# State-space columns from the scaled input while the shift vector loads, and B matrices loaded by group

## The chip, the core and the metric

The kernel runs on one core of a Trainium2 chip as one launch. The metric is the device time of one execution, in microseconds (us); less is better. The engines go by their short names: PE is TensorE (matmuls and transposes; PEld its weight loads), DVE is VectorE, ACT is ScalarE, POOL is GpSimd, and SP is SyncE, which issues most of the DMAs. Weights lie in HBM in f32 and are read through SBUF; matmuls write to PSUM.

## The reference

Two transformer blocks for 256 tokens of width 2048. The change touches the first. Its input is normalised, scaled by `1 + sc1` and shifted by `sh1`; both vectors are a product of the condition vector with 2048 columns of `w_ada`. The projection `w_in` gives u (1024 columns, for the state-space branch), then q, k, v and two gates. Cut to that:

```python
mod = c_act @ w_ada[l] + b_ada[l]
sh1, sc1, g1, sh2, sc2, g2 = [m[:, None, :] for m in jnp.split(mod, N_MOD, axis=-1)]
h = rms_norm(x, norm_mix_g[l]) * (1.0 + sc1) + sh1
proj = h @ w_in[l]
u, q, k, v, ga, gb = jnp.split(proj, split_at, axis=-1)
y_ssm = s5_branch(u, ...)       # per group of 16 columns: B u, a diagonal recurrence over 256 tokens, C s, GLU
y_att = moba_attention(q, k, v, rel_bias)
merged = sigmoid(ga) * (y_ssm @ w_proj_ssm[l]) + sigmoid(gb) * (y_att @ w_proj_attn[l])
x = x + g1 * (merged @ w_out[l])
h2 = rms_norm(x, norm_mlp_g[l]) * (1.0 + sc2) + sh2
x = x + g2 * (jnp.square(jax.nn.relu(h2 @ w_ff1[l])) @ w_ff2[l])
```

The state-space branch has 64 groups with 64 states and 16 columns each; its B matrices `ssm_b_re` and `ssm_b_im` are 64 x 64 x 16.

## The kernel before

**Layout.** Activations stand transposed, features on the 128 partitions and the 256 tokens along a row, in 16 chunks of 128 features. `xT` (two tiles of 8 chunks, in pairs `xp`) is the input so.

**GEMMs.** `gemm` walks the 2048 rows of a weight in steps of 4 chunks by 512 columns: one 1 MB tile `w` per step. `piece` loads it and splits it in two f32r parts, `wh` by ACT (a rounding copy) and `wl` by DVE (the rest). The activations are split in the same way (`h1h`, `h1l`; for the GLU `zhh`, `zhl`). Each product is three matmuls (high by high, high by low, low by high) into PSUM tiles `ga` or `gb`, which ACT evicts (`store_pairs`).

**Conditioning vectors.** `ada_pe` computes one on PE: 16 chunks of 1 MB (`aw`), each times the condition vector repeated over 32 columns (`crep`), four matmuls of 512 columns a chunk, which the hardware runs as eight, into `adap`. `ada` does the same on DVE, in an accumulator `acc`. `ada_fin` copies the sum (`adae`), transposes it (`adat`) and adds bias and gain into `mod`.

**Order.** Up to `pinned[0] = False` (L921) each engine keeps the program's order. From there the tile scheduler orders by its own simulation of the engines. Work beside the GEMMs stands in two lists of generators: `work` (state space, attention) and `stream` (later conditioning vectors). After each part of a GEMM step `bg(dve, ada)` gives credits, 3.6 us of DVE work and 0.65 of a chunk per step of 4 chunks (`TUNE` d1 and r1), and takes the next pieces of the two lists.

**The prologue.** SP issues the chunks of sc1 (`g_sc1`). After the tenth chunk's place in the queue stand the two B loads (L317) and two C loads (L320) into `ssrc`, with runs of 16 f32 for B. `x_in` transposes x on PE (`xt`), DVE copies it to `xT`; the sum of squares gives `rstd`. `ssm_prep` computes the state-space coefficients (`ws`, transposed in `ptp` to `prm`), then rotation tables 0, 1 and 2 (`ssm_table`, doubling steps ln = 1 to 64 into `tab`) with `ssm_blocks` for the four column pairs (`bd`, `cd`, transposed in `pb` and `pc` to `bct`) behind table 0. `columns` brings gains and biases into `colT`. `rr` is the relative-position bias, `bf` its reversed form. After sc1 come the 16 chunks of sh1, during which `mod_scale` writes `xT` times sc1 and rstd; then `mod_shift` makes `h1`.

**The main phase.** The GEMMs follow: u in two halves of 512 columns (L946), q, k, v, a gate, the attention projection, the other gate, and the GLU of the state-space output. `ssm()` starts behind u (L949): for each of 16 pairs of tiles PE makes `bu` from `uT` and `bct`, DVE rotates it with the table, scans along the tokens and rotates back (`wr`, `wi`, `p`), PE sums over the states into `yp`, DVE adds to `uT`, and ACT applies gelu and splits it to `zhh`.

Of the kernel before, what the change touches and what calls it, by code (L numbers as in the profile page):

```python
# [79 lines left out]
def tile_kernel(ctx: ExitStack, tc: tile.TileContext, I, out):  # L80
# [40 lines left out]
    def unit(shape, name="u", dt=F32):  # L121
        return up.tile(shape, dt, name=nm(name), tag="U")

    def scr(shape, name="s", dt=F32):
        return sp.tile(shape, dt, name=nm(name), tag="S")

    def tiny(shape, name="t", dt=F32):
        return tp.tile(shape, dt, name=nm(name), tag="T")
# [6 lines left out]
    def pmisc(shape, name="m"):  # L135
        return psb.tile(shape, F32, name=nm(name), tag="B")
# [175 lines left out]
    g_sc1 = ada_pe(1, 1, "norm_mix_g", crep, pacc_, True)  # L312
    src = unit([P, 4, 512], "ssrc")

    def load_src():
        for k, n in enumerate(("ssm_b_re", "ssm_b_im")):
            SY.dma_start(src[:, k, :].rearrange("p (t q) -> p t q", t=32),  # L317
                        I[n][0].rearrange("(t g) n q -> (g n) t q", g=2))
        for k, n in enumerate(("ssm_c_re", "ssm_c_im")):
            SY.dma_start(src[:, 2 + k, :].rearrange("p (c n) -> p c n", c=8),  # L320
                        I[n][0].rearrange("(c g) q n -> (g q) c n", c=8))
# [105 lines left out]

    def mod_scale(xp, rstd, a, c, dst):
        V.scalar_tensor_tensor(dst, xp[c // 2][:, c % 2, :], a[:, c:c + 1], rstd, op0=OP.mult, op1=OP.mult)

    def mod_shift(t, sh, c, hl):
        S.activation(hl.hi(c), t, AF.Identity, bias=sh[:, c:c + 1])
        V.scalar_tensor_tensor(hl.lo(c), t, sh[:, c:c + 1], hl.hi(c).bitcast(F32),
                               op0=OP.add, op1=OP.subtract)

    def modulate(xp, rstd, a, sh, hl, keep=None, then=None):
        n, ts, lag = 2 * len(xp), {}, 3
        for i in range(n + lag):
            if i < n:
                ts[i] = scr([P, L], "mt") if keep is None else keep[i // 8][:, i % 8, :]  # L440
                mod_scale(xp, rstd, a, i, ts[i])
            c = i - lag
            if c >= 0:
                mod_shift(ts[c], sh, c, hl)
                if c in (3, 7) and then is not None:
                    then()

# [166 lines left out]
    def ssm_prep():  # L614
# [64 lines left out]
        V.tensor_copy(prm, pt)  # L679
        yield 0.2  # L680
        yield from ssm_table(0)
        for pp in range(2):
            bc = unit([P, 2, 2, 512], "bct")
            for k in range(2):
                cp2 = 2 * pp + k
                bct[cp2] = [bc[:, k, i, :].rearrange("p (r c m) -> p r c m", r=2, c=2) for i in range(2)]
                yield from ssm_blocks(cp2, src)
        for cp2 in range(1, 3):
            yield from ssm_table(cp2)

# [182 lines left out]
    xp = pairs_of(xT)  # L873
    r0 = []

    def x_in():
        st = tiny([P, 2], "xst")
        junk = unit([P, D], "xsq")
        for t in range(2):
            S.activation(junk, xtok[t], AF.Square, accum_out=st[:, t:t + 1])  # L880
        for c2 in range(8):
            pt = pmisc([P, 2, L], "xt")
            for k in range(2):
                for t in range(2):
                    T.transpose(pt[:, k, t * P:(t + 1) * P],
                                xtok[t][:, (2 * c2 + k) * P:(2 * c2 + k + 1) * P], ident)
            V.tensor_copy(xp[c2], pt)
            yield 0.6
        r = rsqrt_of(st, 1.0 / D, 2)
        yield 1.0  # L890
        rs = scr([P, L], "rstd")
        S.copy(rs, spread([r[:, t:t + 1] for t in range(2)], pmisc([P, L], "rows")))
        r0.append(rs)
        yield 0.1

    g_x = start(x_in())
    g_ssm = start(ssm_prep())
    g_col = None
    for i, _ in enumerate(g_sc1):
# [8 lines left out]
        bg(2.5, 0)  # L908
    rstd = r0[0]
    start(moba_flip())  # L910
    h = HL(16, "h1")
    for i, _ in enumerate(ada_pe(1, 0, None, crep, pacc_, True)):
        if i < NC:
            mod_scale(xp, rstd, mods[(1, 1)], i, xp[i // 2][:, i % 2, :])
        bg(2.3, 0)
    pre = []
    for c in range(NC):
        mod_shift(xp[c // 2][:, c % 2, :], mods[(1, 0)], c, h)
        if c in (3, 7):
            pre.append(piece(I["w_in"][0], c - 3, 4, 0, 512))  # L920
    pinned[0] = False  # L921

    def queue_ada(*specs, pe=False):
# [9 lines left out]

    w_in = I["w_in"][0]
    for j, g_ in ((2, None), (4, "norm_mlp_g"), (3, None), (5, None)):
        queue_ada((1, j, g_), pe=str(j) in TUNE["pe"])

    def store_pairs(dst, base, func=AF.Copy, scale=1.0):
# [3 lines left out]
        return ev  # L942

    uT = unit([P, 8, L], "uT")
    for nb in range(2):
        gemm(w_in, NC, nb * 512, [("A", 512, store_pairs([uT], 4 * nb))], h, rate=TUNE["r1"], dve=TUNE["d1"], pre=pre if nb == 0 else ())  # L946

    drain(g_ssm)
    g_ssm = start(ssm())  # L949

# [59 lines left out]
    for nb in range(2):  # L1010
        gemm(w_in, NC, 1024 + nb * 512, [("A", 512, store_pairs([qT], 4 * nb, scale=SCALE))], h, rate=TUNE["r1"], dve=TUNE["d1"])
    for nb in range(2):
# [66 lines left out]
    def then(w, n0=0, nn=512):  # L1079
        return lambda: pre.append(piece(w, 4 * len(pre), 4, n0, nn)) if len(pre) < 2 else None  # L1080
# [742 lines left out]
```

## Time and profile before

| | |
|---|---|
| time, median of 3 runs | 3319.54 us (3318.26 to 3321.86) |
| the profiled execution | 3320.44 us |
| its span in the trace | 3318.7 us |
| mean granted PE clock | 0.975 |
| busy: PE, DVE, ACT, POOL | 89%, 68%, 29%, 25% of the span |
| read from HBM | 1064 MB, 321 GB/s over the span |

The first block takes about the first third of the span. [...] A stage is read by what has no idle time in it; an engine's idle time elsewhere costs nothing. Durations of neighbours on one engine overlap by a little, so that from start to start they are shorter than the duration shown.

### The profile page before, as it was taken

The numbers are of one execution on the slowest core, as the hardware profiler recorded it, in microseconds if no ns is written. First come the engines' busy times: TensorE is split into PE (matmuls) and PEld (weight loads), VectorE is DVE, ScalarE is ACT, GpSimd is POOL, SyncE is SP. The second block draws the span as 40 slices with busy tenths as digits, with TensorE's granted clock in tenths as the row PEclk, the third lists the DMA queues.
The fourth block names the chain that finished last, engine by engine and source line by source line (L and its number), as shares of the span: only waits on it lengthen the run. The fifth ranks groups of instructions, "written<-read, shape, count | busy, mean of one in ns | idle before, by whom it ended". The sixth has DMA issues, their size and how long they took to land.

```text
span 3318.7 us, 39085 instructions
## 1 busy us (share of the span) xinstructions
PE 2966.0 (89%) x15580; PEld 2151.7 (65%) x15580; DVE 2268.4 (68%) x3360; ACT 951.7 (29%) x1271; POOL 817.5 (25%) x540
## 2 busy tenths in 40 slices
PE   6899999999999999999999998988877768777777
PEld 2687889998998889997999886444322223222222
DVE  7687689877788888877766647545655565555642
ACT  1323433444443343345336731111111101111000
POOL 1000000000000000000000005556666666666663
PEclk8899999999999999999999998999999989999999
DMA  9866667877899999984883448999999999999998
GB/s 367 303 224 212 208 228 239 300 273 241 285 328 336 328 335 328 328 288 155 280 273 115 153 165 358 419 418 420 421 422 421 422 422 421 422 421 421 422 421 340
DMA packets 280459, 1068.90 MB, mean 322 GB/s; under 512 B 27380, under 2 KB 35991, under 8 KB 189525
## 3 DMA queue, kind: packets, MB, share of 16 engines
q1 hardware_dynamic: 202306, 524.35, 45.8%
q0 software_dynamic: 74752, 538.26, 39.1%
q10 hardware_dynamic: 3220, 3.81, 0.4%
q8 instruction: 122, 2.00, 0.2%
q14 instruction: 59, 0.48, 0.0%
HBM read 1064.24 MB, written 2.11 MB: 321 GB/s over the span
## 4 chain that ended last, share of the span: by engine, by line
PE 61%; DMA 29%; DVE 5%; issue 2%; POOL 1%; ACT 1%; SPq 0%; POOLq 0%; ACTq 0%; DVEq 0%
PE ga L94 31%; DMA dn<-in_peer_down_dram,eid 24%; PE gb L94 18%; PE pe L94 4%; DMA up<-in_peer_up_dram,eid 3%; DVE dn L94 2%; PE adap L94 2%; DMA aw<-in_w_ada_dram 2%; PE xt L94 1%; PE bu L94 1%; PE yp L94 1%; PE wqp L94 1%; PE o L94 1%; DMA up<-in_peer_up_dram,er 1%; POOL dn L1689 1%
## 5 line engine op out<-in xcount | busy, mean ns | idle before, releaser
L94 PE MATMUL pe<-up,cdg 128*128 128x512 f32 x1792 | 831.7, 613 | 258.9 <-DMA up<-in_peer_up_dram,eid 189.4
L1689 POOL DMA_INDIRECT dn<-in_peer_down_dram,eid x256 | 499.4, 1951 | 2256.4 <-DVE g L94 1969.3
L94 DVE SCALAR_TENSOR_TENSOR dn<-dn,htok 128x2048 f32<-128x2048 f32 x256 | 586.0, 2291 | 482.5 <-DMA dn<-in_peer_down_dram,eid 482.4
L94 PEld LDWEIGHTS pe<-up,cdg 128*128 128x128 f32 x1792 | 336.5, 195 | 744.0 <-issue 510.7
L94 ACT ACTIVATE wh<-w 128x2048 fp32r<-128x2048 f32 (+1 forms) x284 | 538.9, 1897 | 876.3 <-PE ga L94 488.5
L94 DVE TENSOR_TENSOR wl<-w,wh 128x2048 fp32r<-128x2048 f32 (+1 forms) x284 | 643.1, 2265 | 193.0 <-ACT wh L94 144.2
L1689 POOL DMA_INDIRECT up<-in_peer_up_dram,eid x224 | 266.5, 1190 | 155.6 <-issue 51.5
L94 DVE SCALAR_TENSOR_TENSOR acc<-aw,cT,acc 128x2048 f32<-128x2048 f32 x105 | 246.6, 2348 | 48.1 <-DMA aw<-in_ada_w_dram 29.9
L94 PE MATMUL ga<-h2h,wh 128*128 128x256 f32 x1024 | 249.1, 283 | 0.0
L94 PE MATMUL ga<-h2l,wh 128*128 128x256 f32 x1024 | 248.6, 283 | 0.0
L94 PE MATMUL ga<-h1h,wh 128*128 128x256 f32 x896 | 224.1, 289 | 0.0
L94 PE MATMUL ga<-h1l,wh 128*128 128x256 f32 x896 | 220.4, 284 | 0.0
L94 PE MATMUL gb<-wh,ah 128*128 128x512 f32 x512 | 199.6, 390 | 0.0
L94 PE MATMUL gb<-wh,al 128*128 128x512 f32 x512 | 199.4, 390 | 0.0
L94 PEld LDWEIGHTS ga<-h2h,wh 128*128 128x128 f32 x1024 | 196.5, 192 | 1.9 <-issue 1.7
L94 PEld LDWEIGHTS ga<-h2l,wh 128*128 128x128 f32 x1024 | 196.5, 192 | 0.2
L94 PEld LDWEIGHTS ga<-h1h,wh 128*128 128x128 f32 x896 | 172.7, 193 | 19.5 <-issue 15.3
L94 ACT ACTIVATE cdg<-ca,cf 128x128 f32<-128x128 f32 x224 | 77.0, 393 | 356.4 <-PE pe L94 345.9
L94 PEld LDWEIGHTS ga<-h1l,wh 128*128 128x128 f32 x896 | 172.9, 193 | 0.9 <-issue 0.8
L94 PE MATMUL ga<-h2h,wl 128*128 128x256 f32 x1024 | 134.1, 283 | 0.0
L94 PE MATMUL ga<-h3l,wh 128*128 128x256 f32 x528 | 132.1, 288 | 0.0
L94 PE MATMUL ga<-h3h,wh 128*128 128x256 f32 x528 | 132.0, 288 | 0.0
(444 smaller groups left out, 4327.4 us busy)
## 6 DMA issues: line engine op xcount, KB each, us to landing
w<-in_w_ff_dram SPq DMA_DIRECT2D x128, 1024.0 KB, 6.6
w<-in_w_in_dram SPq DMA_DIRECT2D x100, 1024.0 KB, 5.6
aw<-in_w_ada_dram SPq DMA_DIRECT2D x96, 1024.0 KB, 7.2
aw<-in_ada_w_dram SPq DMA_DIRECT2D x96, 1024.0 KB, 6.3
w<-in_w_out_dram SPq DMA_DIRECT2D x32, 1024.0 KB, 5.1
wq<-in_peer_wq_dram SPq DMA_DIRECT2D x16, 1024.0 KB, 10.2
w<-in_w_proj_attn_dram SPq DMA_DIRECT2D x8, 1024.0 KB, 5.0
w<-in_w_proj_ssm_dram SPq DMA_DIRECT2D x8, 1024.0 KB, 5.7
```

The costliest lines, as they stand in the source:

```text
L94: r = f(*a, **k)
L1689: r = G.indirect_dma_start(out=rows_, out_offset=None, in_=table, in_offset=bass.IndirectOffsetOnAxis(ap=idx, axis=0))
```

## The change

1. **B matrices.** Both are loaded by group into `raw` (64 partitions, 4 KB contiguous in each). 32 f32 matmuls for each, against a permuted identity, move it to the layout of `ssrc` in PSUM (`sb`), and an ACT copy brings it there.
2. **Input.** `rstd` is computed first and multiplied in when `xt` is taken from PSUM. `mod_scale` is gone.
3. **sh1** (`ada_both`): even chunks are accumulated by DVE (`acc`), odd ones on PE; a product of `acc` with ones adds the two.
4. **u** is taken while sh1 loads: eight 1 MB tiles `wu` of `w_in`'s first 1024 columns, in f32, times `xT` scaled by sc1 and not yet shifted. The f32r GEMM of u is gone.
5. **`u_shift`**, at the head of `stream`: the same columns are loaded again in eight tiles and multiplied by the shift vector `shrep`; the 1024 sums are added to `uT` by ACT.
6. `ssm_prep` makes tables 0 and 1 only; `ssm()`, which makes the others, starts behind q. During q the stream's rate is 1.0.

```diff
+    raw = unit([64, 2, 1024], "raw")
 
     def load_src():
         for k, n in enumerate(("ssm_b_re", "ssm_b_im")):
-            SY.dma_start(src[:, k, :].rearrange("p (t q) -> p t q", t=32),
-                        I[n][0].rearrange("(t g) n q -> (g n) t q", g=2))
+            SY.dma_start(raw[:, k, :], I[n][0].rearrange("g n q -> g (n q)"))
...
-    def mod_scale(xp, rstd, a, c, dst):
-        V.scalar_tensor_tensor(dst, xp[c // 2][:, c % 2, :], a[:, c:c + 1], rstd, op0=OP.mult, op1=OP.mult)
...
+        par = ident[0:64, 0:64].rearrange("p (t g) -> p g t", g=2)
+        for k in range(2):
+            ps = pmisc([P, 32, 16], "sb")
+            rv = raw[:, k, :].rearrange("g (n q) -> g n q", q=16)
+            for q in range(16):
+                for g in range(2):
+                    T.matmul(ps[64 * g:64 * g + 64, :, q], rv[:, :, q], par[:, g, :], start=True, stop=True,
+                             skip_group_check=True)
+            S.copy(src[:, k, :], ps.rearrange("p t q -> p (t q)"))
+            yield 0.1
         yield from ssm_table(0)
...
-        for cp2 in range(1, 3):
-            yield from ssm_table(cp2)
+        yield from ssm_table(1)
...
+        r = rsqrt_of(st, 1.0 / D, 2)
+        rs = scr([P, L], "rstd")
+        S.copy(rs, spread([r[:, t:t + 1] for t in range(2)], pmisc([P, L], "rows")))
+        yield 1.0
...
-            V.tensor_copy(xp[c2], pt)
+            V.tensor_mul(xp[c2], pt, rs.unsqueeze(1).to_broadcast([P, 2, L]))
...
+    uT = unit([P, 8, L], "uT")
+    def ada_both(blk, j, g):
+        dest = const([P, 16], "mod")
+        ps = pacc_([P, 512], "adap")
+        acc = unit([P, D], "acc")
+        for kc in range(NC):
+            wt = rot_tile("aw")
+            SY.dma_start(wt, adaw[blk][kc * P:(kc + 1) * P, j * D:(j + 1) * D])
+            if kc == 0:
+                V.tensor_scalar(acc, wt, ccol[blk][:, 0:1], None, op0=OP.mult)
+            elif kc % 2 == 0:
+                V.scalar_tensor_tensor(acc, wt, ccol[blk][:, kc:kc + 1], acc, op0=OP.mult, op1=OP.add)
+            for l, r in [(crep[:, kc, :], wt)] * (kc % 2) + [(ones[:, 0:32], acc)] * (kc == NC - 1):
+                for q in range(4):
+                    T.matmul(ps[32 * q:32 * q + 32, :], l, r[:, 512 * q:512 * q + 512], start=(kc == 1),
+                             stop=(r is acc), skip_group_check=True)
+            yield 0.0
+        ada_fin(blk, j, ps, dest, g)
+        yield 0.2
+    g_sh1 = ada_both(1, 0, None)
+    def u_load(nb, k):
+        wt = rot_tile("wu").rearrange("p (c n) -> p c n", c=4)
+        SY.dma_start(wt, w_in[4 * k * P:(4 * k + 4) * P, nb * 512:nb * 512 + 512]
+                     .rearrange("(c p) n -> p c n", p=P))
+        return wt
+    for i in range(8):
+        nb, k = divmod(i, 4)
+        wt = u_load(nb, k)
+        if k == 0:
+            ups = [pmisc([P, 2, L], "up") for _ in range(2)]
+        for d in (0.3, 2.3):
+            next(g_sh1)
+            bg(d, 0)
+        if i == 7:
+            for _ in g_sh1:
+                pass
+        for kk in range(4):
+            c = 4 * k + kk
+            if nb == 0:
+                xx, a_ = xp[c // 2][:, c % 2, :], mods[(1, 1)][:, c:c + 1]
+                if kk % 2:
+                    S.activation(xx, xx, AF.Copy, scale=a_)
+                else:
+                    V.tensor_scalar(xx, xx, a_, None, op0=OP.mult)
+            for j in range(4):
+                T.matmul(ups[j // 2][:, j % 2, :], wt[:, kk, j * P:(j + 1) * P], xp[c // 2][:, c % 2, :],
+                         start=(c == 0 and j % 2 == 0), stop=(c == NC - 1), skip_group_check=True)
+        if nb == 0 and k == 3:
+            for j in range(2):
+                S.copy(uT[:, 2 * j:2 * j + 2, :], ups[j])
     h = HL(16, "h1")
-    for i, _ in enumerate(ada_pe(1, 0, None, crep, pacc_, True)):
-        if i < NC:
-            mod_scale(xp, rstd, mods[(1, 1)], i, xp[i // 2][:, i % 2, :])
-        bg(2.3, 0)
     pre = []
     for c in range(NC):
         mod_shift(xp[c // 2][:, c % 2, :], mods[(1, 0)], c, h)
         if c in (3, 7):
-            pre.append(piece(I["w_in"][0], c - 3, 4, 0, 512))
+            pre.append(piece(w_in, c - 3, 4, 1024, 512))
...
+    def u_shift():
+        rep = scr([P, NC, 32], "shrep")
+        V.tensor_copy(rep, mods[(1, 0)].unsqueeze(2).to_broadcast([P, NC, 32]))
+        ps = pmisc([P, 512], "adap")
+        for k in range(8):
+            wt = wp.tile([P, 2, 1024], F32, name=nm("wu"), tag="W")
+            SY.dma_start(wt, w_in[2 * k * P:(2 * k + 2) * P, 0:1024].rearrange("(c p) n -> p c n", p=P))
+            for c in range(2):
+                for q in range(2):
+                    T.matmul(ps[32 * (2 * c + q):32 * (2 * c + q) + 32, :], rep[:, 2 * k + c, :],
+                             wt[:, c, 512 * q:512 * q + 512], start=(k == 0), stop=(k == 7),
+                             skip_group_check=True)
+            yield 0.0
+        ev = scr([P, 512], "adae")
+        S.copy(ev, ps)
+        pt = pmisc([P, 4, P], "adat")
+        for b in range(4):
+            T.transpose(pt[:, b, :], ev[:, 128 * b:128 * b + 128], ident)
+        two = tiny([P, 2, 2, 4], "us")
+        V.tensor_copy(two, pt.rearrange("p b (c q r) -> p c q b r", c=2, q=2)[:, :, :, :, 0])
+        b8 = tiny([P, 8], "ub")
+        V.tensor_add(b8.rearrange("p (q b) -> p q b", q=2), two[:, 0], two[:, 1])
+        for c in range(8):
+            S.activation(uT[:, c, :], uT[:, c, :], AF.Identity, bias=b8[:, c:c + 1])
...
+    g_us = u_shift()
+    stream.append(g_us)
...
-    uT = unit([P, 8, L], "uT")
-    for nb in range(2):
-        gemm(w_in, NC, nb * 512, [("A", 512, store_pairs([uT], 4 * nb))], h, rate=TUNE["r1"], dve=TUNE["d1"], pre=pre if nb == 0 else ())
-
-    drain(g_ssm)
-    g_ssm = start(ssm())
...
-        gemm(w_in, NC, 1024 + nb * 512, [("A", 512, store_pairs([qT], 4 * nb, scale=SCALE))], h, rate=TUNE["r1"], dve=TUNE["d1"])
+        gemm(w_in, NC, 1024 + nb * 512, [("A", 512, store_pairs([qT], 4 * nb, scale=SCALE))], h, rate=1.0,
+             dve=TUNE["d1"], pre=pre if nb == 0 else ())
+    drain(g_us, g_ssm)
+    g_ssm = start(ssm())
```

On PE in the prologue, before (`xt` are the transposes of x, `adap` a chunk of sc1, `rr` the position bias):

```order
L94 MATMUL ptp_283<-ca_81,ws_130 128x32 x5
L94 MATMUL xt_290<-ca_81,xtok_85 128x128
...
L94 MATMUL adap_142<-aw_315,crep_96 32x512 x4
L94 MATMUL xt_321<-ca_81,xtok_85 128x128
...
L94 MATMUL rr_341<-hot_98,rb_100 8x512
L94 MATMUL xt_348<-ca_81,xtok_85 128x128
```

and now:

```order
L94 MATMUL ptp_296<-ca_81,ws_130 128x32 x5
L94 MATMUL xt_303<-ca_81,xtok_85 128x128
...
L94 MATMUL sb_309<-ca_81,raw_136 64x32 x32
L94 MATMUL xt_343<-ca_81,xtok_85 128x128
...
L94 MATMUL adap_143<-aw_349,crep_96 32x512 x4
L94 MATMUL sb_355<-ca_81,raw_136 64x32 x32
L94 MATMUL xt_389<-ca_81,xtok_85 128x128
...
L94 MATMUL rr_395<-hot_98,rb_100 8x512
```

The 32 matmuls for each B matrix (a row of 32 each) stand between the x transposes, ahead of `rr`.

On DVE at the same place, where `prm` are the transposed coefficients and `tab` is table 0, before:

```order
L94 COPY xT_140<-xt_277 128x512
L94 COPY prm_136<-ptp_283 128x160
L94 COPY xT_140<-xt_290 128x512
L94 MEMSET tab_296 128x8 x2
L94 COPY el_299<-prm_136 128x16
L94 TENSOR_TENSOR ta_301<-tab_296,el_299 128x8
...
L94 COPY xT_140<-xt_321 128x512
...
L94 COPY rrs_343<-rr_341 8x512
```

and now:

```order
L94 TENSOR_TENSOR xT_140<-xt_290,rstd_163 128x512
L94 COPY prm_137<-ptp_296 128x160
L94 TENSOR_TENSOR xT_141<-xt_303,rstd_163 128x512
L94 TENSOR_TENSOR xT_141<-xt_343,rstd_163 128x512
L94 TENSOR_TENSOR xT_141<-xt_389,rstd_163 128x512
L94 COPY rrs_397<-rr_395 8x512
L94 MEMSET tab_402 128x8 x2
L94 COPY el_405<-prm_137 128x16
L94 TENSOR_TENSOR ta_407<-tab_402,el_405 128x8
```

Table 0 began ahead of the last x copies and of `rrs`; now it stands behind them, and these take what PE does behind the two `sb` rows.

On PE where the GLU begins (`ga` from `h1` belongs to the last gate, `ga` from `zhh` and `zhl` to the GLU, `yp` is the state-space output, `bu` its input), before:

```order
L94 MATMUL yp_4723<-p_756_5443,bct_559 32x256
L94 MATMUL yp_4723<-p_789_5797,bct_559 32x256
L94 MATMUL ga_5878<-h1h_704,wl_5882 128x256 x5
L94 MATMUL ga_5877<-h1h_704,wh_5937 128x256
...
L94 MATMUL ga_5877<-h1h_705,wl_6052 128x256 x8
L94 MATMUL ga_5878<-h1h_705,wl_6052 128x256 x8
L94 MATMUL ga_6121<-zhh_6109,wh_6125 128x256
```

and now:

```order
L94 MATMUL bu_5844<-uT_773,bct_628 128x256 x2
L94 MATMUL ga_5573<-h1h_1082,wl_5798 128x256 x8
L94 MATMUL ga_5921<-zhh_5909,wh_5925 128x256
...
L94 MATMUL yp_5165<-p_782_5769,bct_628 32x256
...
L94 MATMUL ga_6048<-zhh_5909,wl_6053 128x256 x8
L94 MATMUL yp_5165<-p_797_5885,bct_628 32x256
...
L94 MATMUL yp_5165<-p_799_5890,bct_628 32x256
L94 MATMUL ga_5921<-zhh_5909,wh_5984 128x256
```

The last `yp` stood about a hundred `ga` ahead of the GLU; now the last seven stand inside it, and the last `bu` right ahead of it.

## Rows read from the trace of the kernel before

**Rows 1.** Of the page: the chain that ended last, by engine, shares of the span
```profile
PE 61%; DMA 29%; DVE 5%; issue 2%; POOL 1%; ACT 1%; SPq 0%; POOLq 0%; ACTq 0%; DVEq 0%
```

**Rows 2.** By stage: from:to, length, busy (xinstructions) of each engine, clock, DMA, GB/s
```profile
33.00:40.50 7.50, 6.78 (x23) 2.56 (x24) 5.95 (x33) 0.00 (x0) 0.00 (x0) 0.50 0.96 124
75.40:113.70 38.30, 27.76 (x148) 5.87 (x140) 34.97 (x159) 6.89 (x12) 0.00 (x0) 0.77 0.99 399
113.70:168.20 54.50, 54.50 (x427) 49.60 (x424) 25.25 (x22) 23.32 (x24) 0.00 (x0) 0.96 0.77 254
168.20:640.50 472.30, 472.30 (x3460) 409.27 (x3459) 383.62 (x685) 161.78 (x152) 0.00 (x0) 1.00 0.69 230
```

**Rows 3.** Timeline, SyncE's DMA queue: start, duration, what (xcount)
```profile
18.98 15.97 SPq L317 DMA_DIRECT2D ssrc<-in_ssm_b_im_dram  x1
```

**Rows 4.** Timeline, VectorE, up to the scale vector: start, duration, what, [idle before]
```profile
36.01 0.08 DVE L94 MEMSET tab<- 128x8 f32 x2
...
48.23 0.42 DVE L94 TENSOR_TENSOR ta<-tab,el 128x256 f32<-128x256 f32 x1 [0.28 <-PE rows L94]
...
51.07 0.69 DVE L94 TENSOR_TENSOR ta<-tab,el 128x512 f32<-128x512 f32 x1
...
55.37 0.28 DVE L94 COPY colT<-pt 128x128 f32<-128x128 f32 x1
...
72.18 0.17 DVE L94 COPY el<-prm 128x16 f32<-128x16 f32 x1
...
75.05 0.17 DVE L94 TENSOR_TENSOR mod<-adat,colT 128x16 f32<-128x16 f32 x1 [1.39 <-PE adat L94]
75.26 0.17 DVE L94 SCALAR_TENSOR_TENSOR mod<-mod,colT 128x16 f32<-128x16 f32 x1
```

**Rows 5.** Timeline, TensorE, prologue and shift stage
```profile
26.34 1.06 PE L94 MATMUL adap<-aw,crep 128*32 128x512 f32 x8 [0.83 <-DMA aw<-in_w_ada_dram]
...
34.21 1.11 PE L94 MATMUL xt<-ca,xtok 128*128 128x128 f32 x4
35.25 1.94 PE L94 MATMUL adap<-aw,crep 128*32 128x512 f32 x8
...
38.17 1.87 PE L94 MATMUL rr<-hot,rb 33*8 33x512 f32 x2
...
84.17 1.98 PE L94 MATMUL bf<-rev,ca 128*128 128x512 f32 x4
```

**Rows 6.** TensorE by form: busy us, mean ns, idle before
```profile
L94 PE MATMUL wqp<-hf,wq 128*128 128x256 f32 x512 | 114.9, 381 | 1.1 <-ACT pq L94 0.7 <-ACT scs L94 0.5
...
L94 PE MATMUL hst<-ones,hsq 128*128 128x1 f32 x48 | 5.6, 242 | 0.0
```

**Rows 7.** VectorE by form
```profile
L94 DVE TENSOR_SCALAR acc<-aw,cT 128x2048 f32<-128x2048 f32 x7 | 9.0, 1281 | 0.9 <-DMA aw<-in_ada_w_dram 0.9
```

**Rows 8.** Timeline, VectorE, the end of the state-space recurrence
```profile
584.62 2.29 DVE L94 TENSOR_TENSOR wl<-w,wh 128x2048 fp32r<-128x2048 f32 x1
586.82 0.69 DVE L94 TENSOR_TENSOR wr<-wr,sa 128x512 f32<-128x512 f32 x1
...
605.36 0.46 DVE L94 TENSOR_TENSOR_SCAN wr<-prm,zin,wr 128x128 f32<-128x128 f32 x1
...
610.47 2.35 DVE L94 SCALAR_TENSOR_TENSOR acc<-aw,cT,acc 128x2048 f32<-128x2048 f32 x1
...
621.02 0.87 DVE L94 SCALAR_TENSOR_TENSOR uT<-uT,colT,yp 128x256 f32<-128x256 f32 x2 [0.73 <-PE yp L94]
```

**Rows 9.** Timeline, ScalarE, the same stretch
```profile
627.22 0.61 ACT L94 ACTIVATE uT<-uT 128x512 f32<-128x512 f32 x1
627.86 0.63 ACT L94 ACTIVATE zhh<-uT 128x512 fp32r<-128x512 f32 x1
```

**Rows 10.** Timeline, TensorE, in the GLU GEMM
```profile
640.32 0.28 PE L94 MATMUL ga<-zhh,wh 128*128 128x256 f32 x1
640.44 0.28 PE L94 MATMUL ga<-zhl,wh 128*128 128x256 f32 x1
```

More of the change, by code (lines that the diff above doesn't have):

```diff
@@ L434, in mod_shift @@
                                op0=OP.add, op1=OP.subtract)
[L436 to L446, printed above, removed]
     def gate_rows(dst, c_):
@@ L873, in tile_kernel @@
     xp = pairs_of(xT)
-    r0 = []
     def x_in():
@@ L886, in x_in @@
                                 xtok[t][:, (2 * c2 + k) * P:(2 * c2 + k + 1) * P], ident)
-            V.tensor_copy(xp[c2], pt)
+            V.tensor_mul(xp[c2], pt, rs.unsqueeze(1).to_broadcast([P, 2, L]))
             yield 0.6
[L889 to L894, printed above, removed]
+    w_in = I["w_in"][0]
     g_x = start(x_in())
@@ L908, in tile_kernel @@
         bg(2.5, 0)
-    rstd = r0[0]
     start(moba_flip())
+    uT = unit([P, 8, L], "uT")
[17 more added lines that the diff above has]
+        yield 0.2
@@ L919, in tile_kernel @@
         if c in (3, 7):
-            pre.append(piece(I["w_in"][0], c - 3, 4, 0, 512))
+            pre.append(piece(w_in, c - 3, 4, 1024, 512))
+        if c == 3:
+            for j in range(2):
+                S.copy(uT[:, 4 + 2 * j:6 + 2 * j, :], ups[j])
     pinned[0] = False
+    def u_shift():
[22 more added lines that the diff above has]
+            S.activation(uT[:, c, :], uT[:, c, :], AF.Identity, bias=b8[:, c:c + 1])
+        yield 0.0
     def queue_ada(*specs, pe=False):
@@ L932, in need @@
             cred[0] -= step(stream, False)
-    w_in = I["w_in"][0]
+    g_us = u_shift()
+    stream.append(g_us)
     for j, g_ in ((2, None), (4, "norm_mlp_g"), (3, None), (5, None)):
```

## The prediction

> **What bounds the kernel now.** I read the chain of waits on the page first: TensorE holds 61% of it, DMA 29%, VectorE (DVE) 5% [rows 1]. The DMA share belongs to the second block's gathers, which the change does not touch. So I cut the part it does touch into stages [rows 2]. From 168.2 us (the q GEMM starts) to 640.5 us (the GLU GEMM has just begun) TensorE is busy all 472.30 us at clock 1.00, with DMA at 0.69: more matmuls there are more time. The u GEMM, 113.7 to 168.2, is just as full. The shift stage ahead of it (75.4 to 113.7) is a load: DMA 0.99, TensorE busy 27.76 of 38.30 us. Moving u into that stage is what could pay. At 33 to 40.5 us the load runs at 124 GB/s with its engines busy 0.96 of the time: there the state-space B matrices are read in small runs [rows 2, 3].
>
> The stage up to sc1 ends on a chain through DVE. Table 0 of the rotations starts at 36.01 and ends at 55.37, then come the column vectors and the four state-space block sets until 72.18, table 1's first step, a wait of 1.39 us for the transposed scale vector, and sc1 at 75.43 [rows 4]. The marks of before are thus: sc1 75.4, first u matmul 113.7, first q matmul 168.2.
>
> I sum against the profiled execution, 3320.44 us (1.7 us outside its span). That is 0.9 us above the median, so the difference found goes on the median.
>
> **1. B matrices by group, until sc1.** The two B loads become contiguous. At 399 GB/s, the 7.5 us would have moved 3.0 MB and moved 0.93 MB: some 5 us of load are saved. I count that at nothing, since DVE ends last: its table 0 stands in program order behind the position coefficients, the xT copies and the eight-row copy that follow the new transposes (the DVE rows in the section on the change). TensorE serves these in order: B transposes, four x transposes, an adap chunk, B transposes, four x transposes, the rr matmul. The new raw tile is queued behind ten 1 MB chunks. The sixth is used at 26.34 [rows 5]; four more at 2.6 us (1.05 MB at 399 GB/s) and a quarter MB make 37. With S for one set of B transposes, xt 1.1, adap 1.5 (between 1.06 and 1.94), S, xt 1.1 and rr 1.87 [rows 5], rr ends near 42.5 + 2S. Then come 0.7 for its copy, 0.6 for the xT copy, table 0 at 14.4 (19.4 before, less 5.0 for three copies, the reciprocals and waits that stood between its steps), and 20.1 from the column vectors to sc1 as before (75.43 − 55.37), less the 1.6 us wait for the columns, which will long have landed: sc1 at 76.7 + 2S.
>
> 2S is 64 f32 matmuls of 64 rows by 32 columns, which the hardware runs as 128. No row shows that shape. The nearest is hst, one column against 128x128 weights, 5.6 us for 48, 0.117 each [rows 6]. Half the weight columns at full clock would be 0.06 each, 7.5 us in all; the upper end is twice hst for the half clock at which this stretch runs (0.50, [rows 2]), 0.234 each, 30 us. I take 0.085, 11 us, between hst and its half, the nearest row of the shape. So sc1 comes at 88, 12 us late.
>
> The new matmuls read their weights at a stride of 64 bytes and write PSUM at the same stride. [...]
>
> **2. The shift stage with u inside.** Between sc1 and the first u matmul DVE does four of table 1's seven steps: 14.4 less the first (1.5, from 72.18 to the wait) and the last two (2.8 and 4.3, 48.23 to 55.37 [rows 4]), so 5.8. Then come the first product of the new accumulator (1.28, [rows 7]) and the scaling of two chunks (0.7): 8 us, in which the first adap and bf are hidden. u itself is 128 f32 matmuls of 128x256. The same form is the router's wqp: 114.9 us for 512 hardware matmuls, 0.2244 each [rows 6], and 256 of those are 57.5. Beside them on TensorE: 7 adap chunks at 0.99 (6.9; 1.06 at the full clock less an overlap of 0.07), the ones product (1.0), three bf at 1.0 (3.0) [rows 5], the copy and transposes of the shift vector (1.7), about 1 for a start at the low clock. Sum 79 us. The mod_scale work (16 at 0.48) and 8 of the 16 shift chunks on TensorE go, but both lay beside the load. DMA has 24 MB to bring, 8 of them ahead of the stage: 63 us at 399 GB/s, 42 of them inside, so it no longer ends last. The first q matmul starts at 88 + 79 = 167 against 168.2. The u GEMM of 54.5 us is thus gone, and the stage and the late sc1 have taken its time.
>
> **3. From q to the GLU.** TensorE keeps its 472.3 us and gets 13 chunks more: 8 of the shift product u_shift, which reads w_in's u columns once more, and 5 stream chunks which before stood in the u GEMM. At 0.99 that is 12.9, and 0.7 for one more transpose of a vector: 485.9. The 8 MB more are hidden (DMA share 0.69). So the GLU's start is at 653 + the wait below, 12.5 later. Each us of sc1 passes through one to one.
>
> **4. The wait at the GLU.** The state-space recurrence starts 64 GEMM steps ahead of the GLU before, and 56 now, and carries one table more. Its last two sets reach DVE so late that the order has the last yp matmuls between GLU matmuls, where before some 100 matmuls of the gate GEMM stand between them and the GLU (PE rows in the change). From the second last bu to the last uT DVE has, in row order: 24 products of 512 elements at 0.61 (14.6), 5 wl at 2.20 (11.0), 3 accumulations at 2.26 and one at 1.28 (8.1), 16 scans at 0.38 (6.1), 2 for the small ones: 41.8 [rows 7, 8]; each is its duration less the 0.08 that neighbours overlap, as from wl's start at 584.62 to the next at 586.82. Then yp 2.1, uT 0.9, gelu and zhh 0.63 each [rows 9]: 46. TensorE has 248 ga at 0.12 from start to start [rows 10] (29.8), bu 1.9, transposes 0.7 and the yp 2.1: 34.5. It waits 11.6 us, more by whatever DVE is already behind when the set begins (up to 8: six products, a wl and three zhl stand there first). I take 13; lower end 0, if the scheduler's order has more slack in fact than by these rows.
>
> **Sum.** −1.2 (q start) + 13.6 (chunks in the GEMMs) + 13 (wait) = +25.4 us. On the median: 3345. Later stages are GEMMs and gathers with the same loads and matmuls; conditioning vectors that end late in the first block could add 0 to 4, which I leave out.
>
> **Rivals.** A. *The load's gain counts* (faster). If the B transposes hide in TensorE's waits for chunks, sc1 comes with the load, at 75.4 − 5 = 70. If u is also hidden better, at 73 us of stage (between 79 and the 67 of the matmuls, chunks and ones product alone), q starts at 143 and the GLU at 629, 11.6 earlier, and with no wait there the time is 3308. The point from which it decides: the q start plus the wait under 154.6. For it: TensorE waits for loads in the prologue (0.83 before the sixth chunk [rows 5]), and u's 57.5 us fall in a stage with 10.5 idle. Against: the DVE rows, where table 0 stands behind the transposes. B. *No wait at the GLU*: +12.5, 3332. For it: DVE has 89 us idle in the GEMM stage (383.62 busy of 472.30, [rows 2]). Against: these idles are spread. C. *Dear B transposes*: 2S = 30, sc1 at 107, +44.5: 3364. [...] D. *The early sc1 alone*: sc1 at 70 with the stage of 79 and the GLU's wait of 13: q at 149, −19.2 + 13.6 + 13 = +7.4, 3327; for and against as under A.
>
> **How the numbers follow.** Forecast 0.46 (all slower), A 0.15 (0.14 faster, 0.01 within 0.2%), B 0.17 (0.15 slower, 0.02 within), C 0.12 (slower), D 0.10 (0.06 within, 0.04 slower). Faster by over 0.2% (about 6.6 us, what a measurement tells from no change) 0.14, within 0.09, slower 0.77. Range: below it takes in B and D down to a wait of 4 (3318), leaving out A; above it takes in C with a wait of 20 (3371), 3372. The forecast's own range, from 2S 7.5 with a wait of 6 to 2S 18 with a wait of 20, is 3334 to 3360.
>
> **What would show it.** sc1's mod row on DVE near 88, with table 0 starting near 54 behind xT; the sb matmuls at 0.085 each; the first q matmul at 167, u matmuls at 0.224; TensorE waiting at the GLU for yp, whose DVE products end last. Wrong if sc1 comes at 76 or earlier, if the sb matmuls take over 0.2, if no wait stands before the last yp, or if a later stage moves by more than 4 us.

## The result, and the profile after

The change makes the kernel slower: 3353.76 us, the median of 4 runs (3352.09 to 3355.12), against 3319.72 (also 4 runs, 3318.26 to 3321.86). That is a ratio of 1.0103 with a 95% interval of 1.0089 to 1.0116, or 34 us. The profiled execution took 3352.09 us, its span is 3350.3, 31.6 above the span before.

The stages of the changed kernel, cut at its own marks (sc1 at 90.7, the first u matmul at 98.4, the first q matmul at 171.6, the first GLU matmul at 654.2, the GLU's last at 695.2), answer to [rows 2]; columns as there, the clock as the granted share of the full one:

```profile
33.00:40.50 7.50, 0.98 (x16) 0.82 (x16) 0.98 (x4) 0.00 (x0) 0.00 (x0) 0.56 1.10 265
90.70:98.40 7.70, 1.61 (x11) 0.33 (x3) 7.22 (x43) 1.39 (x3) 0.00 (x0) 0.80 0.62 174
98.40:171.60 73.20, 70.58 (x338) 52.36 (x338) 30.06 (x44) 10.87 (x20) 0.00 (x0) 0.97 0.75 271
171.60:654.20 482.60, 482.60 (x3537) 409.95 (x3534) 366.47 (x731) 167.17 (x168) 0.00 (x0) 1.00 0.69 231
654.20:695.20 41.00, 30.92 (x212) 27.20 (x211) 27.54 (x40) 13.45 (x15) 0.00 (x0) 0.79 0.50 174
```

In the kernel before, the last two stages were these (its u GEMM ended at 168.2, the GLU ran from 638.6 to 661.9):

```profile
168.20:638.60 470.40, 470.40 (x3444) 407.37 (x3443) 382.02 (x684) 160.57 (x150) 0.00 (x0) 1.00 0.69 229
638.60:661.90 23.30, 23.30 (x196) 23.30 (x195) 16.15 (x10) 13.01 (x15) 0.00 (x0) 1.00 0.88 327
```

q starts 3.4 us later than before (171.6 against 168.2). From there to the GLU TensorE is full in both, and 12.2 us longer (482.6 against 470.4). The GLU takes 41.0 us instead of 23.3, 17.7 more. These three sum to 33.3; the rest of the program gives 1.7 back.

VectorE up to sc1, answering to [rows 4]:

```profile
44.67 0.69 DVE L94 TENSOR_TENSOR xT<-xt,rstd 128x512 f32<-128x512 f32 x1 [10.66 <-PE xt L94]
...
51.52 0.69 DVE L94 TENSOR_TENSOR xT<-xt,rstd 128x512 f32<-128x512 f32 x1 [6.15 <-PE xt L94]
...
53.32 0.68 DVE L94 COPY rrs<-rr 8x512 f32<-8x512 f32 x1 [1.11 <-PE rr L94]
53.95 0.07 DVE L94 MEMSET tab<- 128x8 f32 x1
...
56.23 0.69 DVE L94 TENSOR_TENSOR xT<-xt,rstd 128x512 f32<-128x512 f32 x1 [0.82 <-PE xt L94]
...
60.87 0.20 DVE L94 TENSOR_TENSOR tb<-tab,el 128x32 f32<-128x32 f32 x1 [2.19 <-PE pt L94]
...
72.78 0.28 DVE L94 COPY colT<-pt 128x128 f32<-128x128 f32 x1
...
90.29 0.18 DVE L94 TENSOR_TENSOR mod<-adat,colT 128x16 f32<-128x16 f32 x1 [0.94 <-PE adat L94]
90.50 0.17 DVE L94 SCALAR_TENSOR_TENSOR mod<-mod,colT 128x16 f32<-128x16 f32 x1
```

Table 0 (the memset of `tab`) starts at 53.95 instead of 36.01. Ahead of it VectorE stands idle for 10.66, 6.15 and 1.11 us, each time for what TensorE makes behind a set of B transposes; the first of these contains TensorE's own wait for the B tile, 6.52 us (below). sc1 comes at 90.67 instead of 75.43.

TensorE in the prologue and at the start of u, answering to [rows 5]:

```profile
39.71 3.88 PE L94 MATMUL sb<-ca,raw 64*64 64x32 f32 x64 [6.52 <-DMA raw<-in_ssm_b_re_dram]
43.52 1.11 PE L94 MATMUL xt<-ca,xtok 128*128 128x128 f32 x4
44.56 1.94 PE L94 MATMUL adap<-aw,crep 128*32 128x512 f32 x8
46.43 4.01 PE L94 MATMUL sb<-ca,raw 64*64 64x32 f32 x64
50.37 1.11 PE L94 MATMUL xt<-ca,xtok 128*128 128x128 f32 x4
51.41 1.87 PE L94 MATMUL rr<-hot,rb 33*8 33x512 f32 x2
...
98.40 9.01 PE L94 MATMUL up<-xT,wu 128*128 128x256 f32 x32 [6.09 <-issue]
...
119.28 3.07 PE L94 MATMUL up<-xT,wu 128*128 128x256 f32 x13 [1.92 <-DVE xT L94]
```

It waits 6.52 us for the first B tile, does a set of transposes (64 hardware matmuls) in 3.88, four x transposes, a chunk, and the second set in 4.01. Behind sc1 it waits 6.09 us before the first u matmul, in which VectorE does table steps and the first accumulation. The profile names no releaser for this wait; experiment 5 shows that it was VectorE's order.

By form on TensorE, answering to [rows 6]:

```profile
L94 PE MATMUL up<-xT,wu 128*128 128x256 f32 x256 | 58.9, 390 | 8.0 <-issue 6.1 <-DVE xT L94 1.9
...
L94 PE MATMUL sb<-ca,raw 64*64 64x32 f32 x128 | 7.9, 300 | 6.5 <-DMA raw<-in_ssm_b_re_dram 6.5
```

The B transposes cost 7.9 us in all, 0.061 each from start to start within a set (3.88 / 64). u cost 58.9, 57.5 of which were forecast.

TensorE in the GLU, answering to [rows 10]:

```profile
658.75 2.08 PE L94 MATMUL ga<-zhh,wl 128*128 128x256 f32 x16
...
671.63 1.07 PE L94 MATMUL yp<-p,bct 128*32 128x256 f32 x4 [6.00 <-DVE p L94]
...
674.49 2.77 PE L94 MATMUL yp<-p,bct 128*32 128x256 f32 x10 [1.80 <-DVE p L94]
...
679.55 0.80 PE L94 MATMUL ga<-zhh,wh 128*128 128x256 f32 x2 [2.29 <-ACT zhh L94]
...
683.43 3.14 PE L94 MATMUL ga<-zhh,wl 128*128 128x256 f32 x16
```

It waits for VectorE's last products twice (6.00 and 1.80 us) and for the last split of the result (2.29), 10.1 in all. It is also busy 30.9 us instead of 23.3, for two reasons. Sixteen `yp` records now lie in this stretch; they moved there from the stretch ahead of it and cost 3.7 us (experiment 2, which moves them back). And the mean granted clock is 0.79 where it was 1.00: it was 1.00 up to the wait of 6.00 us, behind it 0.50 from 671.6 to 677.2 and 0.53 from 679.5 to 686.3, and then 1.00 again. Sixteen `ga` matmuls took 3.14 us there instead of 2.08. What is left of the 7.6 us, some 4, goes to that.

### The profile page after: what moved, and what is told of

It reads as the page before. It is cut to its first block, busy times and chain, and to the rows that moved or that the text cites. A ratio compares the mean times of both kernels' runs of the same rounds, so it can differ in the third digit from the quotient of the medians.

```text
span 3350.3 us, 39139 instructions
## 1 busy us (share of the span) xinstructions
PE 2979.3 (89%) x15592; PEld 2161.9 (65%) x15592; DVE 2262.7 (68%) x3355; ACT 942.2 (28%) x1280; POOL 819.7 (24%) x540
## 4 chain that ended last, share of the span: by engine, by line
issue 61%; DMA 28%; PE 4%; DVE 4%; POOL 1%; ACT 0%; POOLq 0%; DVEq 0%; ACTq 0%
DMA dn<-in_peer_down_dram,eid 26%; PE pe L94 4%; DMA up<-in_peer_up_dram,eid 2%; DVE dn L94 2%; POOL up L1763 1%; POOL dn L1763 0%; DVE rest L94 0%; DVE ix L94 0%; DVE pick L94 0%; DVE oh L94 0%; DVE v L94 0%; DVE o L94 0%; DVE vals L94 0%; DVE pf L94 0%; DVE ee L94 0%
## 5 line engine op out<-in xcount | busy, mean ns | idle before, releaser
L94 ACT ACTIVATE wh<-w 128x2048 fp32r<-128x2048 f32 x276 | 523.6, 1897 | 849.6 <-PE ga L94 405.0
L94 DVE TENSOR_TENSOR wl<-w,wh 128x2048 fp32r<-128x2048 f32 x276 | 625.1, 2265 | 166.2 <-ACT wh L94 143.2
L94 DVE SCALAR_TENSOR_TENSOR acc<-aw,cT,acc 128x2048 f32<-128x2048 f32 x112 | 263.2, 2350 | 73.7 <-DMA aw<-in_w_ada_dram 38.1
L94 PE MATMUL ga<-h1h,wh 128*128 128x256 f32 x768 | 190.8, 287 | 0.0
L94 PE MATMUL ga<-h1l,wh 128*128 128x256 f32 x768 | 187.5, 283 | 0.0
L94 PEld LDWEIGHTS ga<-h1h,wh 128*128 128x128 f32 x768 | 146.8, 191 | 19.8 <-issue 17.2
L94 PEld LDWEIGHTS ga<-h1l,wh 128*128 128x128 f32 x768 | 147.0, 191 | 1.3 <-issue 1.2
```

The costliest lines, as they stand in the source:

```text
L94: r = f(*a, **k)
```

## The experiments

Ratios are to runs of the kernel before in the same set as the experiment; their medians are 3319.8 to 3320.7 us. Where a time is said to be lower than the changed kernel's, it is compared with the 3353.76 us above, which was not measured again in these sets. The marks (sc1, start of q, start of the GLU) are of each kernel's profiled execution.

**1. The B transposes in the middle of table 0.** Theory: VectorE's place in the program order makes sc1 late. Rival: the late B values do.

```diff
-        (both sets of B transposes)
-        yield from ssm_table(0)
+        for n, v in enumerate(ssm_table(0)):
+            yield v
+            if n in (3, 4):
+                put(n - 3)          # one set of B transposes
```

> The changed kernel with the B transposes issued in the middle of table 0 (after its fourth and fifth step), behind all x transposes, instead of ahead of table 0. Theory: sc1 is late (90.7 us against 75.4) because DVE's table 0 stands in program order behind x copies that TensorE makes only behind the two sets of B transposes; with these moved, table 0 starts near 35 again, sc1 comes at 76 to 79, the stages behind it move up one to one, and the time falls by 12 to 15 us, to 3339 to 3342. Rival: sc1 is late because the four state-space block sets need the B values and these land late (39.7 us) and take 7.8 us on TensorE; then sc1 stays at 86 or later and the time falls by under 5 us.

Measured: 3338.54 us (3335.04 to 3340.70), 15.2 below the changed kernel. VectorE there:

```profile
35.92 0.09 DVE L94 MEMSET tab<- 128x8 f32 x2
...
55.16 0.29 DVE L94 COPY colT<-pt 128x128 f32<-128x128 f32 x1 [1.22 <-PE pt L94]
...
73.37 0.17 DVE L94 SCALAR_TENSOR_TENSOR mod<-mod,colT 128x16 f32<-128x16 f32 x1
```

Table 0 starts at 35.92 and sc1 comes at 73.54, 17.1 us earlier; q starts at 156.4 instead of 171.6. The theory holds. The transposes cost as much as before (7.70 us for both sets), and it no longer matters.

**2. More credit for the work beside the GEMMs.** Theory: the GLU waits for the recurrence, which is emitted too late. Rival: VectorE has no room.

```diff
-TUNE = {"r1": 0.65, "d1": 3.6,
+TUNE = {"r1": 0.65, "d1": 4.2,
```

> The changed kernel with the background credit raised from 3.6 to 4.2 us of DVE work per GEMM step (d1). Theory: the wait at the GLU is the state-space recurrence ending late on DVE; with more credit its pieces are emitted earlier, the last yp stand some 180 matmuls ahead of the GLU, the waits of 6.0, 1.8 and 2.3 us there go, and the time falls by 13 to 17 us, to 3337 to 3341. Rival: DVE has no room, and what is moved forward delays the weight splits, so that TensorE waits elsewhere in the GEMMs: a gain of under 5 us and new waits for wl.

Measured: 3339.39 us (3337.98 to 3347.02), 14.4 lower. From q to the GLU, and the GLU:

```profile
172.20:658.50 486.30, 486.30 (x3553) 411.04 (x3550) 377.20 (x760) 167.91 (x169) 0.00 (x0) 1.00 0.69 229
658.50:681.70 23.20, 23.20 (x195) 23.20 (x195) 16.68 (x11) 12.91 (x15) 0.00 (x0) 1.00 0.86 320
```

The GLU is back to 23.2 us at clock 1.00, no wait stands in it, and the GEMMs ahead of it carry the `yp` that left it (486.3 instead of 482.6) without an idle time. The theory holds, and VectorE had the room.

**3. The old B loads in the changed kernel.**

```diff
-            SY.dma_start(raw[:, k, :], I[n][0].rearrange("g n q -> g (n q)"))
+            SY.dma_start(src[:, k, :].rearrange("p (t q) -> p t q", t=32),
+                        I[n][0].rearrange("(t g) n q -> (g n) t q", g=2))
...
-        (both sets of B transposes)
```

> The changed kernel with the two B loads as before (small runs, straight into their place) and no B transposes. Theory: sc1 comes at 75 to 77 as in the kernel before, and the time falls by 13 to 16 us, to 3338 to 3341, though the load runs slower at 33 to 40 us. Rival: the loads by group save some 5 us that the stage behind needs, so that the fall is under 10 us.

Measured: 3342.95 us (3341.30 to 3347.64), 10.8 lower, between the theory's and the rival's numbers. sc1 came at 76.6, 14.1 us earlier than in the changed kernel but 3.0 later than in experiment 1. TensorE waited for chunks of sc1 there:

```profile
48.49 3.53 PE L94 MATMUL adap<-aw,crep 128*32 128x512 f32 x16 [5.08 <-DMA aw<-in_w_ada_dram]
...
56.26 1.94 PE L94 MATMUL adap<-aw,crep 128*32 128x512 f32 x8 [4.24 <-DMA aw<-in_w_ada_dram]
```

The column transposes stand behind that chunk on TensorE, and VectorE waits 3.25 us for them on its way to sc1. So the loads by group are worth some 4 us net of their transposes (3.0 at sc1, 4.4 in the medians of 1 and 3), once the transposes are out of VectorE's way.

**4. The loads by group alone, in the kernel before.** The edit is part 1 of the change.

> The kernel before with the B loads by group and the B transposes ahead of table 0, as in the change, and nothing else of it. Theory: this part alone makes sc1 13 to 15 us late and the time longer by as much less 0 to 5 us for the sh1 load, which now has its chunks earlier: 3328 to 3335. Rival: the sh1 stage is bound by its load and starts from the chunks, not from sc1; then the time stays within 5 us of 3319.7 or falls.

Measured: 3331.48 us (3329.15 to 3334.47), ratio 1.0035 (1.0022 to 1.0047), 11 us above the kernel before. sc1 came at 87.0, 11.6 late. That is the middle of the theory's range, 3328 to 3335, and 11.6 is a little under its 13 to 15 for sc1. This part of the change is a loss by itself where it was put.

**5. The scaling of x first.**

```diff
     for i in range(8):
...
+        (the scaling of the block's four chunks by sc1)
         for d in (0.3, 2.3):
             next(g_sh1)
             bg(d, 0)
...
-        (the scaling of the block's four chunks by sc1)
```

> The changed kernel with the scaling of xT by sc1 emitted ahead of the sh1 chunks and table steps of its block, instead of behind them. Theory: between sc1 (90.7 us) and the first u matmul (98.4) TensorE waits for DVE, which does four table steps and the first accumulation before it scales the first chunk; with the scaling first, u starts under 2 us behind sc1 and the chunk and the bf that filled the gap come later, so the time falls by 5 to 7 us, to 3347 to 3349. Rival: u's start is set by the load of its first weights or of the shift chunks; then the fall is under 2 us and TensorE waits for a DMA.

Measured: 3349.25 us (3347.63 to 3351.89), 4.5 lower. The wait before the first u matmul fell from 6.09 to 1.2 us, and that of 1.92 at the third block went. The first u matmul still stands 4.6 us behind sc1, since a chunk and two `bf` run ahead of it, and q starts at 167.3 instead of 171.6. The theory holds, a little short of its size.

**6. Without the later shift.** From the kernel of experiment 2; u then lacks its shift, so that this kernel serves to price the shift only:

```diff
-    stream.append(g_us)
...
-    drain(g_us, g_ssm)
+    drain(g_ssm)
```

> The kernel of the credit of 4.2 us without the later shift: u_shift is left out (its 8 MB of loads, 32 matmuls, transposes and the ACT additions), so u lacks its shift term. Theory: TensorE is full from q to the GLU and each matmul there costs its time: 8 chunks at 0.99 and one transpose group make 8.5 us less than with it, 3330 to 3332. Rival: the second load of u's columns is what costs (it delays the q weights), then TensorE waits in q's GEMM go too and the fall is 12 us or more; or the chunks fill gaps and the fall is under 4.

Measured: 3336.58 us (3334.13 to 3337.37), only 2.8 below experiment 2. Inconclusive: with less filling work the order changed, 14 of the `yp` records fell back into the GLU, and that took 29.8 us instead of 23.2, with waits of 1.14 and 1.04 for the split of the result. The GLU started 11 us earlier.

**7. The loads by group in the kernel before, with the transposes in the middle of table 0.** The edit is that of 1 on top of 4.

> The kernel before with the B loads by group and the B transposes in the middle of table 0; nothing else of the change. Theory: sc1 comes when it did (75 to 77 us), the chunks of sh1 are loaded some 5 us earlier, and as the sh1 stage ends on its load (DMA 0.99), u starts up to 5 us earlier: 3315 to 3318. Rival: the stage ends on the chain behind sc1 or on the order of the chunks' buffers, and the 7.8 us of transposes on TensorE delay it: 3319 to 3326.

Measured: 3321.41 us (3319.27 to 3325.25), ratio 1.0006 (0.9997 to 1.0015). No gain: sc1 came at 77.0 instead of 75.4, and the GLU started 1.5 us later. The time lies in the rival's range. In the kernel before, the loads by group, with their transposes, gain nothing.

**8. The three repairs together** (1, 2 and 5).

> The changed kernel with all three repairs: B transposes in the middle of table 0, credit 4.2, and scaling ahead of the block's other work. Theory: the three costs are of three stages and add up: 3353.8 less 15.2, 14.4 and 6 makes 3318, between 3314 and 3321, which is about the kernel before; sc1 at 76, q at 150, the GLU at 633 without a wait. Rival: with sc1 early the stage of u is bound by its loads (24 MB from about 60 us on), so that part of the gains is lost: 3322 or more.

Measured: 3317.76 us (3314.74 to 3320.02), ratio 0.9993 (0.9984 to 1.0002): no difference from the kernel before. The repairs add up (15.2 + 14.4 + 4.5 = 34.1, measured 36.0). sc1 came at 74.1, q started at 149.8, the GLU at 636.0.

**9. u in three f32r passes,** on top of 8.

```diff
-        wt = u_load(nb, k)
+        whi, wlo = nxt              # piece(): split of the block's weights, one block ahead
...
+                    h.put2(c - 1, xp[c // 2])       # split of the scaled x
...
-                T.matmul(ups[j // 2][:, j % 2, :], wt[:, kk, j * P:(j + 1) * P], xp[c // 2][:, c % 2, :],
+                T.matmul(o, whi[:, kk, sl], h.hi(c), ...)
+                T.matmul(o, whi[:, kk, sl], h.lo(c), ...)
+                T.matmul(o, wlo[:, kk, sl], h.hi(c), ...)
...
-            wt = rot_tile("aw")
+            wt = wp.tile([P, D], F32, name=nm("aw"), tag="W")
```

> The kernel with the three repairs, but u taken in three f32r passes from split weights and a split scaled x instead of plain f32, with the shift chunks and u weights in the four W buffers only. Theory: f32 costs TensorE 57.5 us of the stage (0.2244 a hardware matmul, two each) where three f32r passes at 0.12 cost 46; VectorE has room for eight weight splits of 2.2 us and the split of x. The stage between sc1 and q falls from 76 to 66 to 70 us and the time to 3308 to 3313, under both kernels. Rival: VectorE (18 us of accumulation, 13 of table, 18 of weight splits, 10 for x) or the loads with half the buffers end last; TensorE waits for wl or DMA inside the stage, which stays at 75 us or more: 3317 to 3330.

Measured: 3337.75 us (3334.51 to 3340.92), 20 above 8. From sc1 to q took 94 us instead of 76. TensorE there (three of its waits for loads):

```profile
103.69 1.07 PE L94 MATMUL adap<-aw,crep 128*32 128x512 f32 x8 [2.02 <-DMA aw<-in_w_ada_dram]
...
115.67 1.46 PE L94 MATMUL adap<-aw,crep 128*32 128x512 f32 x8 [3.10 <-DMA aw<-in_w_ada_dram]
...
141.62 1.07 PE L94 MATMUL adap<-aw,crep 128*32 128x512 f32 x8 [2.92 <-DMA aw<-in_w_ada_dram]
```

```profile
75.50:169.50 94.00, 70.81 (x476) 54.40 (x468) 60.98 (x104) 30.95 (x41) 0.00 (x0) 0.91 0.76 268
```

The rival holds in that TensorE waits for loads inside the stage. DMA is at 0.76, TensorE at 70.8 and VectorE at 61.0 of 94 us: none is full. The time lies above the rival's 3317 to 3330. The edit leaves four tiles to load ahead into instead of eight; that the chunks come late for that reason alone was not tried by itself, since the splits came with it.

**10. Without the later shift, credit 4.6.**

> The changed kernel without u_shift (u lacks its shift term) and a credit of 4.6 us a step, so that the recurrence ends in time although there are fewer steps of filling work; in the run with 4.2 the stretch to the GLU was 13 us shorter, but the GLU itself 7 longer. Theory: what the later shift costs is TensorE time, 8.8 us; against the run with 4.2 and the shift (3339.4) this one comes to 3329 to 3332. Rival: the shift's chunks are paid for by something else that is late at the GLU or behind it (vectors of the second half that end the first block), so that the time stays over 3335.

Measured: 3334.17 us (3332.65 to 3335.18), 5.2 below experiment 2, between the two. The GLU started 9.2 us earlier (649.3 against 658.5), as the theory has it; the feed-forward part only 3.7 (830.6 against 834.3). Between them TensorE waited 7.3 us instead of 4.5 at the residual's transposes, and 1.0 us at the start of the GEMM behind the GLU; what made up the rest of the 5.5 us was not followed. The shift's 8.8 us are thus shown up to the GLU, where no wait stands in either kernel; how much of them a schedule without it would keep stays open.

**11. sh1 all on VectorE,** on top of 8.

```diff
-            elif kc % 2 == 0:
+            else:
                 V.scalar_tensor_tensor(acc, wt, ccol[blk][:, kc:kc + 1], acc, op0=OP.mult, op1=OP.add)
-            for l, r in [(crep[:, kc, :], wt)] * (kc % 2) + [(ones[:, 0:32], acc)] * (kc == NC - 1):
+            for l, r in [(ones[:, 0:32], acc)] * (kc == NC - 1):
```

> The kernel with the three repairs and the 16 chunks of sh1 all accumulated on VectorE instead of every other one on TensorE. Theory: from sc1 to q TensorE ends last (it is full from the first u matmul on), VectorE has some 40 us idle there and the loads reach 0.75; so the seven chunks that leave TensorE after the first (1.0 us each) shorten the stage by 6 to 8 us, 76 to 69, and the time falls from 3317.8 to 3310 to 3312, under both kernels. Rival: VectorE's 36 us of accumulation come late behind table 1 (chunks are released later, loads start later), so that the sum of sh1 ends after the last u block and the stage stays at 75 or more: 3316 to 3322.

Measured: 3317.36 us (3314.83 to 3320.16), ratio 0.9992 (0.9983 to 1.0001), the same as 8. q starts at 150.0. The chunks left TensorE, and a new wait took their place. VectorE and TensorE there:

```profile
100.70 4.74 DVE L94 SCALAR_TENSOR_TENSOR acc<-aw,cT,acc 128x2048 f32<-128x2048 f32 x2 [7.77 <-DMA aw<-in_w_ada_dram]
...
109.65 0.61 DVE L94 TENSOR_SCALAR xT<-xT,mod 128x256 f32<-128x256 f32 x2
```

```profile
110.05 29.77 PE L94 MATMUL up<-xT,wu 128*128 128x256 f32 x128 [5.83 <-DVE xT L94]
```

The scaling of the fourth block stands on VectorE behind two accumulations that waited 7.77 us for a chunk.

**12. All scalings first, and the last u block ahead of the sum of sh1,** on top of 11.

```diff
+        if i == 0:
+            (the scaling of all 16 chunks)
-        for d in (0.3, 2.3):
+        for d in (0.3, 2.3)[:2 - i // 7]:
...
-        if i == 7:
-            for _ in g_sh1:
-                pass
         (the block's matmuls)
+        if i == 7:
+            for _ in g_sh1:
+                pass
```

> The kernel of the run before (three repairs, sh1 all on VectorE) with two orders changed: all 16 chunks of xT are scaled at the start of the stage, and the last u block stands ahead of the ones product that closes sh1, instead of behind it. Theory: in that run the seven chunks did leave TensorE, but a wait of 5.8 us took their place, because the fourth block's scaling stood on VectorE behind accumulations that wait for a chunk's load (7.8 us); without it the u blocks end at about 142 instead of 149, sh1's sum ends near 138 to 141 anyhow, and q starts at 144 to 146 against 150: 3311 to 3314, under both kernels. Rival: the chunks' loads set the end (DMA 0.95 of 110 to 140 us); sh1's sum then ends as late as before, at 142 or later, its tail of copy, transposes and shift stands bare behind it, and the time stays at 3316 to 3320.

Measured: 3313.12 us (3308.22 to 3317.34), ratio 0.9980 (0.9971 to 0.9989): faster than both kernels. TensorE at the end of the stage:

```profile
103.51 34.70 PE L94 MATMUL up<-xT,wu 128*128 128x256 f32 x160
138.14 1.06 PE L94 MATMUL adap<-acc,ones 128*32 128x512 f32 x8
139.91 0.66 PE L94 MATMUL adat<-ca,adae 128*128 128x128 f32 x4 [0.71 <-ACT adae L94]
```

The u blocks run without a wait to 138.1, sh1's sum follows at once, and q starts at 145.5 against 149.8 in 8. The theory holds. The sixteenth chunk of sh1 now stands behind the last u block too. Which of the orders is worth how much, and whether they gain without the accumulation on VectorE, was not tried.

## Why the prediction came out as it did

The sign and the place of the three losses (the late sc1, the chunks in the GEMMs, the wait at the GLU) were forecast, and the time lies within the stated range: 3345 against 3353.8. Step by step:

- **sc1** (forecast 88, measured 90.7). The mechanism, VectorE's order behind the B transposes, is shown by experiments 1 and 4. Its terms erred in both directions. The first B tile was used at 39.7, not 37 (the forecast's own terms make 37.4): the stretch from 33 to 40.5 us still ran at 265 GB/s, not 399, with the two C loads, which the change leaves as they were, under way beside it. That they are the reason was not tried. The B transposes took 7.9 us, not 11. Together these put the `rr` matmul's end at 53.3 against 53.5; that the two errors cancelled is luck. Table 0 then took 18.8, not 14.4 plus 0.6 for the x copy: VectorE waited 0.82 for that copy and 2.19 for a transpose in between.
- **Rival C** fell. At the half clock (0.50 during both sets) the B transposes took 0.061 each, half of what hst takes per matmul with twice the weight columns [rows 6], and hst ran at clock 1.00 (from 1592.6 to 1594.0 and from 1717.0 to 1718.9 us of the kernel before). The measurement decides against the rival's 0.234. Whether the stride of 64 bytes costs anything is not shown, since no run has the same matmul with contiguous weights.
- **The stage with u** (79 forecast, 80.9 measured). The first u matmul came 7.7 us behind sc1 (8 forecast). u took 58.9, where 57.5 and about 1, the author's estimate, for a start at the low clock were counted: the first 32 matmuls took 9.01 us, at a granted clock of 0.50 in the first 3.6 us, and the later blocks 7.1 to 7.2. One wait of 1.92 for a scaling was not forecast; it is the difference.
- **From q to the end of the GLU** (13.6 and 13 forecast, 12.2 and 17.7 measured). These two terms cannot be compared one by one, since the sixteen `yp` records stand ahead of the GLU before and inside it now. Experiment 2, where no wait stands, separates them. There TensorE's work in the two stretches is 15.8 us more than before (486.3 and 23.2 against 470.4 and 23.3). The `adap` matmuls in front of the GLU are 316 instead of 216, 12.5 chunks of eight where 13 were forecast, but they took 45.7 us instead of 30.2, so 1.2 for each chunk where 0.99 was counted. The rest of the 29.9 us, 14.1, is the wait with what it brings: 10.1 of idle time and 4.0 for the lower clock behind it. So the wait term (13) came out near its size, but not by its own terms: the idle time was less than forecast, and the clock was not in the sum. Experiment 2 shows that the whole term goes with the order. Which of the forecast's two reasons made the recurrence late, eight GEMM steps fewer or one table more, was not tried.
- **Sum**: 25.4 forecast, 33.3 to the end of the GLU. Of the difference, 4.6 is q's start (2.7 from sc1, 1.9 from the stage), 2.2 the work in the GEMMs, and 1.1 the wait. The later stages gave 1.7 back.

The gain that was expected of the change is there, but it is small. Experiment 8 takes the avoidable losses away and arrives at the kernel before: 54.5 us of u GEMM and the 38.3 us of the sh1 stage become one stage of 76, which saves some 17, and the GEMMs behind it grow by 16 (486.2 against 470.4) with the shift's chunks and those that u had covered. Only with sh1's accumulation off TensorE and two orders changed (experiment 12) is the kernel faster than before, by 7 us.

## What to carry to other kernels

Where an engine keeps the program's order, what a new step waits for counts for everything that stands behind it. Here 7.9 us of transposes and the 6.5 us for which they waited for their data cost 15 where they stood; in the middle of a table, where the data had landed, the transposes cost nothing that could be measured (experiments 1 and 7). When a stage is taken out of a schedule, the work that it was covering (five chunks, eight GEMM steps' credit for the recurrence) has to be given a new place, or it comes back as a wait at the next join. After each such repair, look for the next instruction in that queue that waits for a load.

## What the runs showed of the hardware

- f32 matmuls with 64 x 64 weights read at a stride of 64 bytes, and 32 columns, took 0.061 us per hardware matmul at clock 0.50.
- Behind a wait of 6.00 us in the GLU the granted clock was 0.50 where it had been 1.00, and sixteen `ga` matmuls took 3.14 us instead of 2.08. Without waits the GLU ran at 1.00 throughout (experiment 2).
- With four instead of eight 1 MB tiles to load ahead into, and with the splits of u's weights beside them, the 24 MB of the stage took 94 us at a DMA share of 0.76, in which TensorE and DMA both had room (experiment 9). With eight tiles and no splits the stage took 76 (experiment 8). Which of the two differences counts is not shown.
